# Unnormalised keys in the delta rule: their norm moved into beta and the values

## The chip, the cores and the metric

The kernel runs on one core of a Trainium2 chip. The metric is the device time of one execution in microseconds (us), from several runs of the same program; the time of a kernel is their median. The profile is one further execution, recorded by the hardware profiler. A core has five engines with a queue each: TensorE (PE, with its weight loads shown as PEld), VectorE (DVE), ScalarE (ACT), GpSimd (POOL) and SyncE (SP), which here issues all transfers to the 16 DMA engines.

## The reference

A hybrid decoder layer for 512 tokens of width 2048 in float32: a sliding-window attention branch and a gated delta-rule branch share one wide input projection, are merged by gates, and pass an output projection. The change concerns the delta rule. It has 16 key heads and 32 value heads (two value heads share a key) of width 128. After a causal convolution of four taps and a SiLU, queries and keys are normalised by their Euclidean length and the recurrence is solved in chunks:

```python
def l2_norm(x):
    xf = x.astype(jnp.float32)
    return xf * lax.rsqrt(jnp.sum(xf * xf, axis=-1, keepdims=True) + EPS)
...
    k_beta = k * beta[..., None]
    v_beta = v * beta[..., None]
    L = jnp.where(strict, jnp.einsum('bhncd,bhnsd->bhncs', k_beta, k) * decay, 0.0)
    t_inv = lax.linalg.triangular_solve(eye + L, ...)
    u = t_inv @ v_beta
    w = t_inv @ (k_beta * jnp.exp(g)[..., None])
...
    def step(S, xs):
        u_c, w_c, qk_c, qd_c, kd_c, gl_c = xs
        v_new = u_c - w_c @ S
        o = qd_c @ S + qk_c @ v_new
        S = S * gl_c[..., None, None] + jnp.swapaxes(kd_c, -1, -2) @ v_new
        return S, o
```

The output of each head is normalised by its root mean square, gated, and projected.

## The kernel before

All work hangs on one stream of weight products. A channel tile (`channel_tile`, L290) is 128 output channels by 512 tokens: 16 slices of the inner dimension, three products each (`mm3`, L270), because every float32 operand is split into a high and a low part in a faster 32-bit format. The weights of a tile (1 MB) are loaded by SP into one of two `raw` buffers (L215); ACT rounds a half of it to the high part (L61), DVE subtracts to get the low part (L62), into one of three buffer pairs `whi`/`wlo`. A half serves 24 products. A load or a split is issued when the buffer before it has been used (`half_done`, `weight_tick`).

All other work is written as Python generators that are advanced beside this stream. Every second slice of a channel tile calls `pump` (L91), one step: it counts down each live generator's delay and runs it to its next `yield`, whose value is the number of steps until it goes on. So a step is six weight products, and the order of instructions on each engine follows from these yields, with small rearrangements by the compiler's scheduler. Each engine runs its instructions in its fixed order; a waiting instruction holds up those behind it.

In the key stage (`delta_keys`, L662) 16 channel tiles give the 16 keys; the first four come out of the startup, the next four follow one another, the last eight alternate with tiles of the merge gate. Each key runs through `keys` (L729): convolution and SiLU give y, channels by tokens; y is transposed to tokens by channels (`transpose4`, L317, PSUM tile `ptk`); ACT sums its squares per token (`sumsq`, L774); DVE computes the inverse root by Newton steps (`rsqrt`, L65); ACT writes the normalised keys k with four scaled copies (L745). k is stored for later (L751), transposed back (`ptkT`, L750), copied by ACT to kT (L753), stored (L761) and multiplied with itself on PE (`pkk`, L760). Meanwhile the decay factors E of both value heads are loaded by a broadcast DMA (L783), masked on POOL (L788) and exponentiated on ACT (L794); DVE multiplies them with the product (L763), and six stores (L770, L771) put the result in DRAM. `ptk`, `ptkT` and `pkk` share two buffers in PSUM.

When eight keys are done, `solve` (L796) loads their triangular systems and the rows of beta, scales the systems by beta, and inverts them on DVE in 62 pairs of paced operations. It runs twice.

In the head stage (`delta_heads`, L697) five channel tiles per key head give one query, two values and two output gates. `queries` (L880) loads k and kT, builds the query-key products, and after waiting for both values runs the recurrence (`scan`, L961) over four blocks of 128 tokens. `values` (L869) convolves, transposes into `ptv` and copies with ACT to `vt` (L877), tokens by channels. `neg_beta` (L629) is minus beta, tokens by heads; `queries` uses it at L952. The stores and loads of SP, in its one queue, carry the weights too.

Of the kernel before, what the change touches and what calls it, by code (L numbers as in the profile page):

```python
# [7 lines left out]
F32 = mybir.dt.float32  # L8
F32R = mybir.dt.float32r
I32 = mybir.dt.int32  # L10
AF = mybir.ActivationFunctionType
# [34 lines left out]
class Layer:  # L46
# [615 lines left out]
    def delta_keys(self):  # L662
        tc = self.tc
        dram = self.dram
        self.lt_d = dram.tile([2, 2, 16, 4, HD, HD], F32, name="lt_d")
        self.lab_d = dram.tile([VH, HD, 4, HD], F32, name="lab_d")
        self.ta_d = dram.tile([2, 16, 4, HD, HD], F32, name="ta_d")
        self.ts_d = dram.tile([2, 2, 16, 4, HD, HD], F32, name="ts_d")
        self.kT_d = dram.tile([KH, P, T], F32, name="kT_d")
        self.k_d = dram.tile([KH, P, T], F32, name="k_d")  # L670
        self.o_d = dram.tile([VH, P, T], F32, name="o_d")
        with ExitStack() as sa:
            self.ptp = sa.enter_context(tc.tile_pool(name="ptp", bufs=2, space=PSUM, reuse_waits="tile"))
            self.gwk = sa.enter_context(tc.tile_pool(name="gwk", bufs=1, reuse_waits="tile"))
            wk = sa.enter_context(tc.tile_pool(name="dnA", bufs=2, reuse_waits="tile"))
            gp = sa.enter_context(tc.tile_pool(name="gates", bufs=1, reuse_waits="tile"))
            self.go(self.gates(gp), 1)
            gt = sa.enter_context(tc.tile_pool(name="gatew", bufs=1, reuse_waits="tile"))
            self.beside(self.gate(gt), 0.26, "gate")
            self.keys_done = []  # L680
            for g in range(NST):
                self.go(self.keys(wk, g, self.acc_k[g]), 10 + 8 * g)
            for j in range(NFIRST):
                self.merge_gate("mb", j, self.mb_d)
            self.solved = []
            self.solves = self.paced(self.solve_all(), 0.36)
            for kind, j in self.mixed():
                if kind == "k":
                    self.go(self.keys(wk, j, self.channel_tile(f"k{j}")), 0)
                else:  # L690
                    self.merge_gate("mb", j, self.mb_d)
            for j in range(2):
                self.merge_gate("ma", j, self.ma_d)
            self.drain("gate")
            self.drain_live()
# [33 lines left out]
    def keys(self, wk, g, ps):  # L729

        nc = self.nc
        y = wk.tile([P, T], F32, tag="y", name="y", bufs=3)
        yield from self.conv(wk, ps, 16 + g, y)
        yield 2
        pt = self.ptp.tile([P, T], F32, tag="tp", name="ptk")
        self.transpose4(pt, lambda c: y[:, c * P : (c + 1) * P])
        ss = self.sumsq(wk, pt)
        yield 3
        E = [self.decay_load(wk, 2 * g + e) for e in range(2)]
        nc.vector.tensor_scalar(out=ss, in0=ss, scalar1=EPS, scalar2=None, op0=ALU.add)  # L740
        rk = self.rsqrt(wk, ss, NTB, "rk")
        yield 4
        k = wk.tile([P, NTB, P], F32, tag="k", name="k")
        for c in range(NTB):
            nc.scalar.activation(k[:, c, :], pt[:, c * P : (c + 1) * P], AF.Copy, scale=rk[:, c : c + 1])  # L745
        for e in range(2):
            self.decay_mask(E[e])
        yield 4
        pt = self.ptp.tile([P, T], F32, tag="tp", name="ptkT")
        self.transpose4(pt, lambda c: k[:, c, :])  # L750
        nc.sync.dma_start(out=self.k_d[g], in_=k.rearrange("p c d -> p (c d)"))  # L751
        kT = wk.tile([P, T], F32, tag="kT", name="kT")
        nc.scalar.copy(out=kT, in_=pt)  # L753
        for e in range(2):
            self.decay_exp(E[e], 2 * g + e)
        yield 2
        pk = self.ptp.tile([P, NTB, P], F32, tag="tp", name="pkk")
        for c in range(NTB):
            sl = slice(c * P, (c + 1) * P)
            nc.tensor.matmul(pk[:, c, :], lhsT=kT[:, sl], rhs=kT[:, sl], start=True, stop=True)  # L760
        nc.sync.dma_start(out=self.kT_d[g], in_=kT)  # L761
        for e in range(2):
            nc.vector.tensor_tensor(out=E[e], in0=pk, in1=E[e], op=ALU.mult)  # L763
        yield 2
        for e in range(2):
            h = 2 * g + e
            b, hl = h // 16, h % 16
            for k2 in range(2):
                s = slice(k2 * HD, (k2 + 1) * HD)
                nc.sync.dma_start(out=self.lt_d[b, k2, hl].rearrange("c j i -> j c i"), in_=E[e][s, :, s])  # L770
            nc.sync.dma_start(out=self.lab_d[h], in_=E[e][0:HD, :, HD:P])  # L771
        self.keys_done.append(g)
# [23 lines left out]
    def solve(self, wk, b, eng):  # L796

        nc = self.nc
        while not all(g in self.keys_done for g in range(8 * b, 8 * b + 8)):
            yield 1.0  # L800
        A = wk.tile([P, HD, HD], F32, tag="A", name="A", bufs=1)
        bet = wk.tile([P, HD], F32, tag="bet", name="bet", bufs=1)
        for k2 in range(2):
            s = slice(k2 * HD, (k2 + 1) * HD)
            nc.sync.dma_start(
                out=A[s].rearrange("u j i -> u (j i)"), in_=self.lt_d[b, k2].rearrange("h c j i -> (h c) (j i)")
            )
            nc.sync.dma_start(
                out=bet[s],
                in_=self.b_rows.rearrange("h (c k i) -> k (h c) i", c=4, k=2)[k2, b * HD : (b + 1) * HD, :],  # L810
            )
        yield 8.0
        nb = wk.tile([P, HD], F32, tag="nbet", name="nbet", bufs=1)
        self.behind(eng.tensor_scalar(out=nb, in0=bet, scalar1=-1.0, scalar2=None, op0=ALU.mult))
        self.behind(eng.tensor_tensor(out=A, in0=A, in1=nb.unsqueeze(1).to_broadcast([P, HD, HD]), op=ALU.mult))
        eng.memset(A.rearrange("u j i -> u (j i)")[:, 0 : HD * HD : HD + 1], 1.0)
        for m in range(1, HD - 1):
            n = HD - 1 - m
            yield 0.1 + 0.00115 * m * n
            tmp = wk.tile([P, 1024], F32, tag="atmp", name="atmp", bufs=1)  # L820
            t = tmp[:, : m * n].rearrange("p (j i) -> p j i", j=m)
            self.behind(
                eng.tensor_tensor(  # L823
                    out=t,
                    in0=A[:, m : m + 1, m + 1 :].to_broadcast([P, m, n]),
                    in1=A[:, :m, m : m + 1].to_broadcast([P, m, n]),
                    op=ALU.mult,
                )
            )
            yield 0.1 + 0.00115 * m * n  # L830
            self.behind(eng.tensor_tensor(out=A[:, :m, m + 1 :], in0=A[:, :m, m + 1 :], in1=t, op=ALU.add))  # L831
        tmp = wk.tile([P, 1024], F32, tag="atmp", name="atmp", bufs=1)
        for q in range(8):
            yield 1.1
            half = tmp[:HD, (q % 2) * 512 : (q % 2 + 1) * 512]
            t = half.rearrange("p (i j) -> p i j", j=HD)
            self.behind(nc.scalar.copy(out=t, in_=A[:HD, :, q * 8 : (q + 1) * 8].rearrange("u j i -> u i j")))
            yield 0.2
            nc.sync.dma_start(
                out=self.ta_d[b].rearrange("h c i j -> (h c) (i j)")[:, q * 512 : (q + 1) * 512], in_=half  # L840
            )
        yield 4.5
        self.behind(eng.tensor_tensor(out=A, in0=A, in1=bet.unsqueeze(2).to_broadcast([P, HD, HD]), op=ALU.mult))
        for k2 in range(2):
            s = slice(k2 * HD, (k2 + 1) * HD)
            nc.sync.dma_start(
                out=self.ts_d[b, k2].rearrange("h c j i -> (h c) (j i)"), in_=A[s].rearrange("u j i -> u (j i)")
            )
# [20 lines left out]
    def values(self, wk, g, e, ps, st):  # L869
        nc = self.nc  # L870
        y = wk.tile([P, T], F32, tag="y", name="yv", bufs=3)
        yield from self.conv(wk, ps, 32 + 2 * g + e, y)
        yield 3
        pt = self.ptp.tile([P, T], F32, tag="tp", name="ptv")
        self.transpose4(pt, lambda c: y[:, c * P : (c + 1) * P])
        vt = wk.tile([P, NTB, P], F32, tag="vt", name="vt", bufs=3)
        nc.scalar.copy(out=vt.rearrange("p c d -> p (c d)"), in_=pt)  # L877
        st[f"v{e}"] = vt

    def queries(self, wk, g, ps, st):  # L880
# [926 lines left out]
```

## Time and profile before

| | us |
|---|---|
| median of 3 runs | 2839.93 |
| lowest and highest run | 2839.35, 2842.86 |
| span of the profiled execution (first to last instruction) | 2839.0 |

The profile gives the span of its execution alone; the fastest of the runs is 0.35 us above that span, the median 0.93. The page begins with each engine's busy time, its share of the span and its count of instructions; matmuls overlap, and their ends are modelled. Section 4 of the page is the chain that ended last: from the last instruction back to whatever released it, and so on to the start, as shares of the span. Rows of a timeline give start, duration, engine, line, operation, output<-inputs and count, and in brackets the idle time before with what ended it. A row of a tile gives the durations as minimum/median/maximum in ns, then the first and the last start in us. A row of the waits gives the total in us, the number of times and the longest.

### The profile page before, as it was taken

To read this page: it belongs to the slowest core of one execution; us is meant where nothing else is said; L and a number is where in the kernel's file an instruction comes from. 1 tells how busy PE (TensorE), PEld (TensorE's weight loads), DVE (VectorE), ACT (ScalarE), POOL (GpSimd) and SP (SyncE) were. 2 spreads that over 40 slices of the span, in tenths; PEclk is the share of its full clock that TensorE was granted. 3 is DMA by queue.
4 is the path that set the end of the run, shared out by engine and by line. 5 is a ranking of instruction groups with operands and counts; after the bars stand their busy time and mean duration, and the time that the engine had idled before them with its cause. 6 is when DMAs were issued, how large, how long until landed. Compare 5 with 4: busy or idle time off the path is not lost.

```text
span 2839.0 us, 38354 instructions
## 1 busy us (share of the span) xinstructions
PE 2806.5 (99%) x14152; PEld 2283.3 (80%) x14152; DVE 1944.8 (69%) x3185; ACT 1207.1 (43%) x2476; POOL 146.0 (5%) x124
## 2 busy tenths in 40 slices
PE   8999999999999999999999999999999999999999
PEld 6788888877776788888888888888888888878887
DVE  7866876867758667778766666666656766664676
ACT  5555443244544443333434333333334454432443
POOL 0010000100000010000001000000000000000000
PEclk9999999999999999999999999999999999999999
DMA  9877764322243253356777667677647886885684
GB/s 402 335 246 230 257 218 139 110 91 91 82 135 119 101 168 110 117 201 219 247 255 262 235 224 242 210 239 238 231 167 252 289 314 240 302 273 180 242 318 168
DMA packets 228512, 603.25 MB, mean 212 GB/s; under 512 B 76354, under 2 KB 102594, under 8 KB 188002
## 3 DMA queue, kind: packets, MB, share of 16 engines
q1 hardware_dynamic: 228324, 600.80, 62.1%
q8 instruction: 111, 1.82, 0.3%
q14 instruction: 77, 0.63, 0.1%
HBM read 480.32 MB, written 118.17 MB: 211 GB/s over the span
## 4 chain that ended last, share of the span: by engine, by line
PE 91%; DMA 3%; DVE 3%; ACT 1%; issue 1%; SPq 0%; POOL 0%; DVEq 0%; ACTq 0%; POOLq 0%
PE mm L273 22%; PE mm L275 21%; PE mm L274 21%; PE m L274 5%; PE m L273 5%; PE m L275 5%; PE pod L1000 1%; PE O L1514 1%; PE pv L981 1%; DVE wlo L62 1%; PE pod L999 1%; PE pod L996 1%; PE pp L971 1%; PE S L1451 1%; DMA wa<-in_w_ada_ss 1%
## 5 line engine op out<-in xcount | busy, mean ns | idle before, releaser
L273 PE MATMUL mm<-hh,whi 128*128 128x512 f32 x2784 | 1130.4, 406 | 1.5 <-ACT hh L61 1.5
L275 PE MATMUL mm<-hh,wlo 128*128 128x512 f32 x2784 | 1090.4, 392 | 0.0
L274 PE MATMUL mm<-hl,whi 128*128 128x512 f32 x2784 | 1087.9, 391 | 0.0
L62 DVE TENSOR_TENSOR wlo<-raw,whi 128x1024 fp32r<-128x1024 f32 x516 | 636.9, 1235 | 426.4 <-ACT whi L61 415.4
L61 ACT CAST whi<-raw 128x1024 fp32r<-128x1024 f32 x516 | 541.3, 1050 | 799.9 <-PE mm L274 566.6
L273 PEld LDWEIGHTS mm<-hh,whi 128*128 128x128 f32 x2784 | 524.0, 188 | 117.0 <-issue 14.3
L275 PEld LDWEIGHTS mm<-hh,wlo 128*128 128x128 f32 x2784 | 523.0, 188 | 113.8 <-issue 0.2
L274 PEld LDWEIGHTS mm<-hl,whi 128*128 128x128 f32 x2784 | 524.7, 188 | 100.9 <-issue 1.6
L1246 DVE TENSOR_TENSOR q<-q,q 128x1024 f32<-128x1024 f32 x96 | 124.8, 1300 | 0.0
L794 ACT ACTIVATE E<-E,neg_g 128x128 f32<-128x128 f32 x256 | 81.2, 393 | 92.3 <-POOL E L788 89.6
L831 DVE TENSOR_TENSOR A<-A,atmp 128x62 f32<-128x62 f32 (+30 forms) x124 | 109.5, 883 | 0.6
L823 DVE TENSOR_TENSOR atmp<-A 128x62 f32<-128x62 f32 (+30 forms) x124 | 107.4, 866 | 0.4
L928 POOL TENSOR_TENSOR qe<-qe,yq 128x512 f32<-128x512 f32 x32 | 54.1, 1708 | 923.9 <-DMA qe<-eg_rows 695.9
L1001 ACT COPY osb<-pod 128x256 f32<-128x256 f32 x64 | 23.8, 372 | 152.6 <-PE pod L1000 152.6
L788 POOL TENSOR_SCALAR_AFFINE_SELECT E<-E 128x512 f32<-128x512 f32 x64 | 59.1, 936 | 431.2 <-DMA E<-g_rows 384.5
L983 ACT COPY vn<-pv 128x256 f32<-128x256 f32 x64 | 23.8, 372 | 124.4 <-PE pv L981 124.4
L652 DVE SCALAR_TENSOR_TENSOR yv<-mm,convh,yv 128x511 f32<-128x511 f32 (+2 forms) x96 | 71.2, 742 | 1.1
L988 DVE TENSOR_SCALAR vs<-vn,kd 128x128 f32<-128x128 f32 x96 | 23.1, 283 | 58.3 <-ACT vn L983 58.3
L1482 ACT ACTIVATE sm<-sm,mx,rs 128x128 f32<-128x128 f32 x128 | 61.5, 482 | 3.4 <-DVE mx L1477 2.3
L1011 DVE SCALAR_TENSOR_TENSOR S<-S,egl,pod 128x128 f32<-128x128 f32 x64 | 19.3, 342 | 51.0 <-ACT junk L1004 51.0
L472 DVE SCALAR_TENSOR_TENSOR wa<-wa,silu_cb 128x2048 f32<-128x2048 f32 x22 | 50.1, 2285 | 4.8 <-DMA wa<-in_w_ada_ss 4.8
L657 ACT ACTIVATE th<-yv 128x512 f32<-128x512 f32 x32 | 20.1, 630 | 76.4 <-DVE yv L652 73.7
(444 smaller groups left out, 3678.8 us busy)
## 6 DMA issues: line engine op xcount, KB each, us to landing
raw<-in_w_ch SPq DMA_DIRECT2D x158, 1024.0 KB
wa<-in_w_ada_ss SPq DMA_DIRECT2D x32, 1024.0 KB
q<-in_w_od SPq DMA_DIRECT2D x64, 512.0 KB
g_d<-q SPq DMA_DIRECT2D x64, 512.0 KB
raw<-g_d SPq DMA_DIRECT2D x32, 1024.0 KB
raw<-in_w_od SPq DMA_DIRECT2D x24, 1024.0 KB
gw<-in_w_ada_gate SPq DMA_DIRECT2D x16, 1024.0 KB
E<-g_rows SPq DMA_DIRECT2D x64, 256.0 KB
```

Source lines behind the costliest of these rows:

```text
L61: h = self.nc.scalar.copy(out=hi, in_=src)
L62: l = self.nc.vector.tensor_tensor(out=lo, in0=src, in1=hi.bitcast(F32), op=ALU.subtract)
L273: nc.tensor.matmul(ps, lhsT=wh, rhs=xh, start=first, stop=False)
L274: nc.tensor.matmul(ps, lhsT=wh, rhs=xl, start=False, stop=False)
L275: self.last_mm = nc.tensor.matmul(ps, lhsT=wl, rhs=xh, start=False, stop=last)
L652: nc.vector.scalar_tensor_tensor(out=y[:, s:], in0=ps[:, : T - s], scalar=w[:, j : j + 1], in1=y[:, s:], op0=ALU.mult, op1=ALU.add)
L788: self.last_mask = self.nc.gpsimd.affine_select(out=E, in_=E, pattern=[[0, NTB], [1, P]], compare_op=ALU.is_ge, fill=NEG, base=0, channel_ ...
L794: self.nc.scalar.activation(E[:, c, :], E[:, c, :], AF.Exp, bias=self.neg_g[:, c, h : h + 1])
L823: eng.tensor_tensor(out=t, in0=A[:, m : m + 1, m + 1 :].to_broadcast([P, m, n]), in1=A[:, :m, m : m + 1].to_broadcast([P, m, n]), op=ALU.mult,
L831: self.behind(eng.tensor_tensor(out=A[:, :m, m + 1 :], in0=A[:, :m, m + 1 :], in1=t, op=ALU.add))
L1246: self.behind(nc.vector.tensor_tensor(out=q[f], in0=q[x], in1=q[y], op=ALU.add))
L1482: nc.scalar.activation(t, t, AF.Exp, scale=r[:, h : h + 1], bias=mx[:, h : h + 1], accum_out=den[:, h : h + 1])
```

## The change

Keys are no longer divided by their length. With n the length of a key row (n squared is the sum of squares plus EPS), k = y / n. Beta is divided by n squared, and the values are multiplied by n; the solved quantity then comes out divided by n, and with y in place of k all later products are the same as before. In detail:

- `keys`: the scaled copies, the second transposition and its copy go. ACT copies the transposed y unscaled; y itself takes the place of kT in DRAM and in the self product. y gets four buffers, kT none.
- The length n (`knorm`), as sum times inverse root, stays in SBUF for all keys; the inverse of the sum is multiplied into `neg_beta` and stored for both value heads in `inv_d`, by a transfer that scatters single elements into rows of tokens.
- The yields of `keys` after the sum of squares: 3, 2, 2, 2, 2 instead of 3, 4, 4, 2, 2.
- `solve` loads the rows of `inv_d` beside those of beta and multiplies them.
- `values`: four scaled copies instead of one copy.

```diff
+        self.inv_d = dram.tile([VH, T], F32, name="inv_d")
+        self.knorm = self.dnc.tile([P, NTB, KH], F32, name="knorm")
...
     def keys(self, wk, g, ps):
 
         nc = self.nc
-        y = wk.tile([P, T], F32, tag="y", name="y", bufs=3)
+        y = wk.tile([P, T], F32, tag="y", name="y", bufs=4)
         yield from self.conv(wk, ps, 16 + g, y)
         yield 2
         pt = self.ptp.tile([P, T], F32, tag="tp", name="ptk")
         self.transpose4(pt, lambda c: y[:, c * P : (c + 1) * P])
+        nc.sync.dma_start(out=self.kT_d[g], in_=y)
         ss = self.sumsq(wk, pt)
+        k = wk.tile([P, NTB, P], F32, tag="k", name="k")
+        nc.scalar.copy(out=k.rearrange("p c d -> p (c d)"), in_=pt)
         yield 3
         E = [self.decay_load(wk, 2 * g + e) for e in range(2)]
         nc.vector.tensor_scalar(out=ss, in0=ss, scalar1=EPS, scalar2=None, op0=ALU.add)
         rk = self.rsqrt(wk, ss, NTB, "rk")
-        yield 4
-        k = wk.tile([P, NTB, P], F32, tag="k", name="k")
-        for c in range(NTB):
-            nc.scalar.activation(k[:, c, :], pt[:, c * P : (c + 1) * P], AF.Copy, scale=rk[:, c : c + 1])
+        nc.vector.tensor_tensor(out=self.knorm[:, :, g], in0=ss, in1=rk, op=ALU.mult)
+        inv = wk.tile([P, NTB], F32, tag="inv", name="inv")
+        nc.vector.reciprocal(out=inv, in_=ss)
+        both = inv.unsqueeze(2).to_broadcast([P, NTB, 2])
+        nb = self.neg_beta[:, :, 2 * g : 2 * g + 2]
+        nc.vector.tensor_tensor(out=nb, in0=nb, in1=both, op=ALU.mult)
+        nc.sync.dma_start(out=self.k_d[g], in_=k.rearrange("p c d -> p (c d)"))
+        for e in range(2):
+            nc.sync.dma_start(out=self.inv_d[2 * g + e].rearrange("(c p) -> p c", p=P), in_=inv)
+        yield 2
         for e in range(2):
             self.decay_mask(E[e])
-        yield 4
-        pt = self.ptp.tile([P, T], F32, tag="tp", name="ptkT")
-        self.transpose4(pt, lambda c: k[:, c, :])
-        nc.sync.dma_start(out=self.k_d[g], in_=k.rearrange("p c d -> p (c d)"))
-        kT = wk.tile([P, T], F32, tag="kT", name="kT")
-        nc.scalar.copy(out=kT, in_=pt)
+        yield 2
         for e in range(2):
             self.decay_exp(E[e], 2 * g + e)
         yield 2
         pk = self.ptp.tile([P, NTB, P], F32, tag="tp", name="pkk")
         for c in range(NTB):
             sl = slice(c * P, (c + 1) * P)
-            nc.tensor.matmul(pk[:, c, :], lhsT=kT[:, sl], rhs=kT[:, sl], start=True, stop=True)
-        nc.sync.dma_start(out=self.kT_d[g], in_=kT)
+            nc.tensor.matmul(pk[:, c, :], lhsT=y[:, sl], rhs=y[:, sl], start=True, stop=True)
...
         bet = wk.tile([P, HD], F32, tag="bet", name="bet", bufs=1)
+        nb = wk.tile([P, HD], F32, tag="nbet", name="nbet", bufs=1)
...
-            nc.sync.dma_start(
-                out=bet[s],
-                in_=self.b_rows.rearrange("h (c k i) -> k (h c) i", c=4, k=2)[k2, b * HD : (b + 1) * HD, :],
-            )
+            for dst, rows in ((bet, self.b_rows), (nb, self.inv_d)):
+                nc.sync.dma_start(
+                    out=dst[s], in_=rows.rearrange("h (c k i) -> k (h c) i", c=4, k=2)[k2, b * HD : (b + 1) * HD, :]
+                )
         yield 8.0
-        nb = wk.tile([P, HD], F32, tag="nbet", name="nbet", bufs=1)
+        self.behind(eng.tensor_tensor(out=bet, in0=bet, in1=nb, op=ALU.mult))
...
         vt = wk.tile([P, NTB, P], F32, tag="vt", name="vt", bufs=3)
-        nc.scalar.copy(out=vt.rearrange("p c d -> p (c d)"), in_=pt)
+        for c in range(NTB):
+            nc.scalar.activation(vt[:, c, :], pt[:, c * P : (c + 1) * P], AF.Copy, scale=self.knorm[:, c, g : g + 1])
```

## The prediction

> **What bounds the kernel now.** I read the page first, then the windows of the key stage, then PE's timeline in it.
>
> ```profile
> span 2839.0 us, 38354 instructions
> ...
> PE 2806.5 (99%) x14152; PEld 2283.3 (80%) x14152; DVE 1944.8 (69%) x3185; ACT 1207.1 (43%) x2476; POOL 146.0 (5%) x124
> ...
> PE 91%; DMA 3%; DVE 3%; ACT 1%; issue 1%; SPq 0%; POOL 0%; DVEq 0%; ACTq 0%; POOLq 0%
> ```
>
> PE is busy for 2806.5 of 2839.0 us, and the chain that ended last lies on PE for 91%. The change works in the key stage (about 140 to 445 us) and where values leave PSUM in the head stage. In the windows the columns are the length, the busy time (and count) of PE, PEld, DVE, ACT and POOL, PE's clock, the DMA share and GB/s:
>
> ```profile
> 140.00:200.00 60.00, 60.00 (x300) 49.78 (x300) 41.31 (x79) 33.03 (x99) 6.78 (x8) 1.00 0.72 237
> 200.00:260.00 60.00, 58.99 (x296) 48.84 (x295) 39.94 (x92) 39.96 (x120) 6.63 (x9) 1.00 0.72 224
> 260.00:320.00 60.00, 60.00 (x287) 49.95 (x287) 40.45 (x70) 28.38 (x69) 4.26 (x6) 1.00 0.84 266
> 320.00:380.00 60.00, 60.00 (x283) 49.91 (x282) 51.91 (x82) 29.99 (x79) 6.63 (x6) 1.00 0.77 257
> 380.00:445.00 65.00, 65.00 (x301) 52.73 (x301) 44.13 (x67) 25.65 (x60) 4.15 (x6) 1.00 0.52 174
> ```
>
> PE misses only 1.0 us of these 305, at a granted clock of 1.00. So an instruction taken off PE here shortens the run as long as nothing else comes late, and work added to ACT, DVE, SP or the DMA queues costs nothing until PE waits for it.
>
> **What leaves PE.** Each of the 16 keys loses its second transposition, four matmuls of 128x128, 64 in all. The tile's row gives min/median/max in ns; the timeline shows one such group between weight products; the last two rows are the ends of a run without any insertion:
>
> ```profile
> L320 PE MATMUL ptkT<-ident,k x64: 270/273/330, 165.0 to 435.7; 128*128 128x128 f32 x64
> ...
> 290.10 0.39 PE L274 MATMUL mm<-hl,whi 128*128 128x512 f32 x1
> 290.32 0.40 PE L275 MATMUL mm<-hh,wlo 128*128 128x512 f32 x1
> 290.56 0.60 PE L320 MATMUL ptkT<-ident,k 128*128 128x128 f32 x4
> 290.91 0.48 PE L273 MATMUL mm<-hh,whi 128*128 128x512 f32 x1
> 291.23 0.40 PE L274 MATMUL mm<-hl,whi 128*128 128x512 f32 x1
> 291.46 0.39 PE L275 MATMUL mm<-hh,wlo 128*128 128x512 f32 x1
> ...
> 302.42 0.39 PE L275 MATMUL mm<-hh,wlo 128*128 128x512 f32 x1
> ...
> 312.62 0.39 PE L275 MATMUL mm<-hh,wlo 128*128 128x512 f32 x1
> ```
>
> From 302.42 to 312.62 there are 45 products: 10.20 / 45 = 0.227 us from start to start, though each row lasts 0.39 (they overlap). From the L275 at 290.32 to the next at 291.46 are 1.14 us, where three products alone take 0.68. The group therefore costs PE 1.14 - 0.68 = 0.46 us. 16 x 0.46 = **7.4 us** leave PE. I price by the displacement and not by the 273 ns, since neighbours overlap.
>
> The Trainium skill ("TensorE: Matmul & The Clock Gate", Part 4) gives about 275 ns for one PE transposition inside a kernel. The trace agrees on the duration (273); by the page the sum would be 64 x 0.275 = 17.6 us. That is the third rival below.
>
> A second gain is a wait. In this stage PE waits on ACT once:
>
> ```profile
> PE ptk L320 <- ACT k L745: 0.9, 1, 0.9
> ```
>
> The two transposition buffers in PSUM are shared by three tiles per key, and one is held until ACT has scaled it by the root, which DVE must compute first. After the change the copy needs no root and there are two tiles per key: this wait should go, **0.9 us**. What is late next is taken up below.
>
> The products of the keys with themselves (L760) stay, eight entries per key, reading y instead of kT; same shape and count, no cost.
>
> **What is added and moved.** DVE gets three small operations per key (norm, reciprocal, new beta) and one multiplication per solve.
>
> ```profile
> L73 DVE TENSOR_TENSOR rkt<-rkt,ss x48: 149/161/585, 155.6 to 422.7; 128x4 f32<-128x4 f32 x48
> ...
> L1487 DVE RECIPROCAL den<-den x16: 202/203/204, 581.5 to 1002.8; 128x8 f32<-128x8 f32 x16
> ```
>
> 2 x 0.16 + 0.20 = 0.52 us per key, 8.4 us in all, spread over a stage where DVE is at most 51.91 of 60 us busy: hidden. Uncovered it would be those 8.4 us.
>
> ACT loses the copy of the transposed keys and three of the four scaled copies in the key stage, and gets three more per value tile in the head stage:
>
> ```profile
> L753 ACT COPY kT<-ptkT x16: 567/587/606, 166.3 to 436.0; 128x512 f32<-128x512 f32 x16
> ...
> 210.05 1.14 ACT L745 ACTIVATE k<-ptk,rky 128x128 f32<-128x128 f32 x4 [0.98 <-DVE rky L74]
> ...
> 1077.48 0.58 ACT L877 COPY vt<-ptv 128x512 f32<-128x512 f32 x1
> ...
> L981 PEld LDWEIGHTS pv<-vt,tt x40: 187/189/193, 1080.9 to 1693.5; 128*128 128x128 f32 x40
> ```
>
> Four scaled pieces take 1.14 us where one copy takes 0.58, so 32 value tiles cost ACT 32 x 0.56 = 18 us more. The first product that needs a value tile starts at 1080.9, 2.8 us after that copy ended at 1078.06; 0.56 more fits. Hidden; a tile that didn't fit would cost at most 0.56, 18 us at the very worst.
>
> The new order in a key: between the first transposition and the self product lie 9 steps of the generator instead of 13 (3+2+2+2 for 3+4+4+2). The decay factors E keep the time of their load, but mask, exponential and product come 2, 4 and 4 steps sooner.
>
> ```profile
> 298.75 0.60 PE L320 MATMUL ptk<-ident,y 128*128 128x128 f32 x4
> ...
> 305.68 0.91 SPq L783 DMA_DIRECT2D E<-g_rows  x2
> ...
> 312.15 1.30 POOL L788 TENSOR_SCALAR_AFFINE_SELECT E<-E 128x512 f32<-128x512 f32 x2 [19.13 <-DMA E<-g_rows]
> ...
> 315.93 2.46 ACT L794 ACTIVATE E<-E,neg_g 128x128 f32<-128x128 f32 x8
> ...
> 317.63 0.89 PE pkk L760 x8
> ```
>
> 13 steps took 317.63 - 298.75 = 18.9 us, 1.45 each. With 9 the self product stands at 298.75 + 13.1 = 311.8. But the mask waits for the load until 312.15 and ends at 313.45, and eight exponentials take 2.46: E is whole at about 315.9. So DVE would stand at its product for 2 to 4 us, and ACT at its exponential, issued at step 7 (308.9), for some 4 us. Behind them queue the split of the weights (L61 on ACT, L62 on DVE), the next convolution and the solver; PE waits for the split. Its cover:
>
> ```profile
> 306.01 1.05 ACT L61 CAST whi<-raw 128x1024 fp32r<-128x1024 f32 x1 [3.44 <-PE mm L274]
> ...
> 307.10 1.23 DVE L62 TENSOR_TENSOR wlo<-raw,whi 128x1024 fp32r<-128x1024 f32 x1
> ```
>
> The cast waits for PE to free the buffer it just finished, so with three buffers two halves are ready: 2 x 24 x 0.227 = 10.9 us of PE work, and the split is done at 308.33, 2.3 us after the start. A cover of 8.6 us against a delay of 2 to 4. It is thinner where DVE is at 51.91 of 60. I bound PE's new waits by 0 and by 5 us (four keys in 320 to 400 at a good microsecond each) and take **+1.0**, near the only such row there is (0.9).
>
> SP and the queues. The stores of keys move forward; that of the transposed form (L761) now waits for nothing new. Two stores per key are new, 512 runs of 4 bytes each. They are issued right behind DVE's chain, so SP stands there until DVE has run it, with weight loads behind; a load has the same cover.
>
> ```profile
> L751 SPq DMA_DIRECT2D k_d<-k x16: 319/383/601, 164.3 to 425.1; - x16
> ...
> L770 SPq DMA_DIRECT2D lt_d<-E x64: 574/611/1827, 172.7 to 444.1; - x64
> ```
>
> A store of 128 runs is issued in 383 ns, one of 256 runs in 611; carried on, 512 take about 1.1 us (estimate), 2.2 per key. No row shows a 4-byte run written to DRAM. Nearest below is a window with only short reads, nearest above one with 256-byte stores:
>
> ```profile
> DMA packets 307, 0.01 MB, mean 10 GB/s; under 512 B 307, under 2 KB 307, under 8 KB 307
> ...
> q1 hardware_dynamic: 307, 0.01, 14.5%
> ```
>
> ```profile
> DMA packets 933, 0.33 MB, mean 304 GB/s; under 512 B 880, under 2 KB 880, under 8 KB 932
> ...
> q1 hardware_dynamic: 932, 0.32, 115.4%
> ```
>
> The first (461.0 to 462.2) gives 0.145 x 16 x 1.2 us / 307 = 9 ns a run, the second (279.5 to 280.6) 1.154 x 16 x 1.1 / 932 = 22 ns. 1024 runs per key on 16 engines are 0.6 to 1.4 us per key. From 200 to 260 the share is 0.72, so 28% of the time is free; a key comes there with each channel tile at most, 48 x 0.227 = 10.9 us, so 3.1 us are free per key. So it is hidden; I take 9 to 22 ns, because the rows for the shorter and the longer run bracket the size, and keep the other price as the second rival. Two more loads per half in the solver are of 64 rows and lie beside the load of A.
>
> **The sum**, on the execution's span: 2839.0 - 7.4 - 0.9 + 1.0 = 2831.7. The median of the runs, 2839.93, lies 0.9 above the span: **2832.6 us**.
>
> **Rivals.**
> First, the wait moves instead of going: E comes too late for the shorter order, DVE and ACT stall at every key, and where DVE is fullest the split of the weights is late. For it: mask at 312.15 against a product at 311.8. Against it: 8.6 us of cover. At the upper bound, +5: 2836.6.
>
> Second, slower: the 4-byte stores fill the queues, and weights and E come late. It decides from the point where 1024 runs eat the free 3.1 us of a key: 3.1 x 16 / 1024 = 48 ns a run in the dense stretch, and from 80 ns for the whole stage (free by the five windows' shares: 0.28 x 120 + 0.16 x 60 + 0.23 x 60 + 0.48 x 65 = 88 us less the last keys' share, some 82; 16384 runs on 16 engines). At 100 ns the runs take 102 us, 20 over: 2839.9 - 8.3 + 20 = 2852. Against it stand the 9 and 22 ns. The Trainium skill ("DMA: Bandwidth & Descriptors", Specifications) says that transfers under 512 bytes are done by reading, modifying and writing back. It gives no price for it; the trace's 256-byte stores show none at 22 ns, and no row here shows one at 4 bytes.
>
> Third, PE gets back the transpositions' whole duration: 64 x 0.273 = 17.5 us, 2839.9 - 17.5 - 0.9 + 1.0 = 2822.5. The displacement of 0.46 per group speaks against it.
>
> **How the numbers follow.** The forecast (2830 to 2834) has 0.66, the first rival 0.17, the slow one 0.11, the third 0.06. The measurement can tell about 0.2% from no change, 5.7 us: faster is below 2834.3, slower above 2845.6. Faster: 0.66 + 0.06 = 0.72; same 0.17; slower 0.11. The range starts at the forecast without the new wait (2831.6) less 2.6 us, a quarter of the way to the third rival, since single groups may be displaced differently, and ends 2 us above the first rival: 2829 to 2838.5.
>
> **What would show it.** Right: 64 fewer matmuls on PE; busy time of PE lower by about 7; the stage from the first key to the last product of the stage shorter by 7 to 8; no PE wait on ACT at ptk; the value copies at 1.14 us with PE's product still behind them by over 2 us. The first rival: PE waits on wlo or whi between 200 and 440, DVE idle before L763's product. The second: DMA share near 1 there, casts waiting for raw. The prediction is wrong if the stage's PE time falls by 7 and the end doesn't follow, which would mean that something behind this stage sets the end.

## The result and the profile after

The changed kernel takes 2886.2 us (median of 4 runs, 2884.57 to 2891.89) against 2840.21 us (4 runs, 2839.35 to 2842.86) for the kernel before in the same comparison. The ratio is 1.0164, with a 95% interval of 1.0149 to 1.0178: slower by 46 us. I had forecast 2832.6 and given the case that came true, the second rival, a chance of 0.11.

The head of the page of the changed kernel: span, busy time of the engines, PE's clock and the DMA share in 40 slices of 72 us, and the chain that ended last.

```profile
span 2884.0 us, 38324 instructions
...
PE 2809.8 (97%) x14088; PEld 2285.4 (79%) x14088; DVE 1947.6 (68%) x3235; ACT 1209.9 (42%) x2508; POOL 140.0 (5%) x124
...
PEclk9999899999999999999999999999999999999999
DMA  9889998332235243346777767667646887885684
...
PE 84%; DMA 9%; DVE 3%; issue 2%; ACT 1%; SPq 1%; POOL 0%; DVEq 0%; POOLq 0%; ACTq 0%
```

PE has its 64 matmuls fewer (14152 to 14088), yet its busy time is 3.3 us longer, and the chain, which lay on PE for 91%, has 9% on DMA where it had 3%. Both point to one stage. The windows of the key stage after the change (length, then busy time and count of PE, PEld, DVE, ACT, POOL, then PE's clock, DMA share, GB/s):

```profile
140.00:200.00 60.00, 57.52 (x271) 46.79 (x269) 32.15 (x72) 25.54 (x76) 4.95 (x6) 0.97 0.75 170
200.00:260.00 60.00, 41.92 (x181) 34.28 (x180) 31.27 (x84) 23.92 (x65) 3.82 (x6) 0.85 0.89 179
260.00:320.00 60.00, 53.94 (x246) 44.79 (x246) 30.69 (x70) 24.21 (x66) 4.94 (x6) 0.93 0.96 166
320.00:380.00 60.00, 52.78 (x223) 42.86 (x224) 45.78 (x77) 21.48 (x49) 3.17 (x4) 0.88 1.00 239
380.00:445.00 65.00, 55.42 (x249) 45.25 (x247) 44.95 (x72) 25.18 (x59) 4.72 (x6) 0.95 0.99 209
445.00:500.00 55.00, 52.79 (x231) 42.55 (x232) 40.67 (x66) 19.84 (x48) 4.06 (x6) 0.97 0.87 219
```

PE is full at clock 1.00 in the same windows before. Now it misses up to 18 us of 60, and its clock falls to 0.85. The DMA share rises to as much as 1.00, while in the first four windows the bytes per second fall (from 380 us on, the late work is still being loaded). Over the whole stretch from 140 to 500 us no engine but the queues works longer. That stretch as one window, first before, then after:

```profile
140.00:500.00 360.00, 358.99 (x1706) 296.74 (x1706) 253.55 (x429) 176.63 (x448) 28.45 (x34) 1.00 0.66 217
```

```profile
140.00:500.00 360.00, 314.36 (x1398) 256.52 (x1397) 225.51 (x436) 140.17 (x362) 25.67 (x34) 0.92 0.91 197
```

By the durations of their packets the queues are busy for 0.25 x 360 = 90 us longer, and they move a tenth less. PE stands for 45.6 us instead of 1.0, and the trace's clock records give 54.6 us at half clock, where before had none. Matched product by product, the weight products run 54 us later than before's at 490 us, 47 later at 885, and 45 later at the end: the whole loss is made in the key stage, and some 9 us come back afterwards.

PE's waits after the change, from 140 to 500 us (what waited, for what; us in total, times, longest):

```profile
PE ptk L320 <- DVE y L659: 25.6, 6, 8.3
PE ptk L320 <- DVE rky L74: 9.1, 1, 9.1
PE mm L273 <- ACT whi L61: 5.2, 2, 3.2
PE mm L275 <- DVE wlo L62: 3.6, 4, 1.1
```

The list names DVE, yet DVE has less to do than before. The timeline shows who is really late (start, duration, engine, line, operation; in brackets the idle time ahead and what ended it):

```profile
190.81 1.06 SPq L755 DMA_DIRECT2D inv_d<-inv  x2
...
195.06 0.43 SPq L788 DMA_DIRECT2D E<-g_rows  x1
...
206.70 0.64 POOL L793 TENSOR_SCALAR_AFFINE_SELECT E<-E 128x512 f32<-128x512 f32 x1 [10.43 <-DMA lab_d<-E]
...
207.37 0.40 ACT L799 ACTIVATE E<-E,neg_g 128x128 f32<-128x128 f32 x1 [7.43 <-DMA lab_d<-E]
207.67 0.61 ACT L657 ACTIVATE th<-y 128x512 f32<-128x512 f32 x1
208.32 0.69 DVE L659 SCALAR_TENSOR_TENSOR y<-th,y 128x512 f32<-128x512 f32 x1 [6.36 <-ACT th L657]
209.16 1.09 PE L320 MATMUL ptk<-ident,y 128*128 128x128 f32 x4 [9.12 <-DVE rky L74]
...
210.90 0.63 PE L275 MATMUL mm<-hh,wlo 128*128 128x512 f32 x1
```

Read upwards from PE: it stands 9.12 us for y; DVE stands 6.36 for the convolution's tanh; that tanh is queued on ACT behind the exponential of E, which stands 7.43; the exponential needs POOL's mask, which stands 10.43 for E's load. The brackets of the mask and the exponential name the store of `lab_d`, but the semaphore of that load of E, for which the mask also waits, is complete only at 206.40, 0.3 us before the mask. The load was issued at 195.06, and the mask begins 11.6 us later; in the case of before quoted in the prediction it was 6.5 (305.68 to 312.15). The load left SP behind the two stores of 190.81. Nothing on this path computes longer: each engine works in order, so one late load stops all of them.

A second loss follows the stall: the last row lasts 0.63 us where such products lasted 0.39. PE works at half clock after it.

### The profile page after: what moved, and what is told of

Same layout as the page of the kernel before. It is cut to its first block, busy times and chain, and to the rows that moved or that the text cites. A ratio compares the mean times of both kernels' runs of the same rounds, so it can differ in the third digit from the quotient of the medians.

```text
span 2884.0 us, 38324 instructions
## 1 busy us (share of the span) xinstructions
PE 2809.8 (97%) x14088; PEld 2285.4 (79%) x14088; DVE 1947.6 (68%) x3235; ACT 1209.9 (42%) x2508; POOL 140.0 (5%) x124
## 4 chain that ended last, share of the span: by engine, by line
PE 84%; DMA 9%; DVE 3%; issue 2%; ACT 1%; SPq 1%; POOL 0%; DVEq 0%; POOLq 0%; ACTq 0%
PE mm L273 20%; PE mm L275 19%; PE mm L274 19%; PE m L274 5%; PE m L273 5%; PE m L275 5%; DMA gw<-in_w_ada_gate 3%; DMA E<-g_rows 2%; DMA raw<-in_w_ch 2%; PE pv L988 1%; PE pod L1007 1%; PE O L1521 1%; DMA mb_d<-mth 1%; PE pod L1006 1%; PE pod L1003 1%
## 5 line engine op out<-in xcount | busy, mean ns | idle before, releaser
L1717 DVE SCALAR_TENSOR_TENSOR gate_bc<-gw,silu_c,gate_bc 128x2048 f32<-128x2048 f32 x15 | 35.6, 2375 | 26.6 <-DMA gw<-in_w_ada_gate 26.6
```

## The experiments

| run | us, median | before, same chip | ratio (95%) | DMA share 140 to 500 |
|---|---|---|---|---|
| e1_no_scatter | 2824.28 | 2842.02 | 0.9939 (0.9921 to 0.9956) | 0.65 |
| e2_before_scatter | 2891.60 | 2842.02 | 1.0160 (1.0128 to 1.0191) | 0.91 |
| e3_rows_by_pe | 2831.44 | 2842.02 | 0.9964 (0.9952 to 0.9976) | 0.65 |
| e4_old_yields | 2900.15 | 2842.02 | 1.0205 (1.0186 to 1.0225) | 0.90 |
| e5_one_store | 2900.61 | 2840.53 | 1.0209 (1.0193 to 1.0226) | 0.89 |
| e6_runs_16 | 2843.80 | 2840.53 | 1.0009 (1.0000 to 1.0019) | 0.69 |
| e7_runs_apart | 2845.14 | 2840.53 | 1.0016 (1.0006 to 1.0025) | 0.70 |
| e8_rows_old_yields | 2847.99 | 2840.53 | 1.0026 (1.0016 to 1.0037) | 0.65 |
| e9_rows_paused | 2845.75 | 2838.45 | 1.0023 (1.0012 to 1.0034) | 0.66 |
| e10_runs_16_bytes_apart | 2848.16 | 2838.45 | 1.0032 (1.0020 to 1.0044) | 0.78 |
| e11_change_runs_apart | 2831.33 | 2840.07 | 0.9971 (0.9960 to 0.9982) | 0.75 |

**Is it the stores, and are they enough?** Two kernels from both ends: the changed kernel without its stores, and the kernel before with nothing but them.

e1_no_scatter, against the changed kernel:

```diff
-        for e in range(2):
-            nc.sync.dma_start(out=self.inv_d[2 * g + e].rearrange("(c p) -> p c", p=P), in_=inv)
...
-            for dst, rows in ((bet, self.b_rows), (nb, self.inv_d)):
+            for dst, rows in ((bet, self.b_rows),):
...
-        self.behind(eng.tensor_tensor(out=bet, in0=bet, in1=nb, op=ALU.mult))
+        self.behind(eng.tensor_scalar(out=bet, in0=bet, scalar1=0.001, scalar2=None, op0=ALU.mult))
```

> The changed kernel without the 32 scattering stores of 4-byte runs; the solver multiplies beta by 0.001 in place of the loaded inverse, so its result is another. Everything else of the change stays: the shorter order, the unscaled copy, the scaled values. Theory S (the scattering stores hold the DMA queues, and weights and E come late): about 2832 us, PE idle under 3 us between 140 and 500 us, DMA share near 0.66 there. Theory O (the shorter order and the moved stores stall ACT, DVE and SP whatever the stores cost): about 2880 us, PE idle still some 45 us.

e2_before_scatter, against the kernel before, behind the root of a key (nothing reads what it stores):

```diff
+        self.inv_d = dram.tile([VH, T], F32, name="inv_d")
...
         rk = self.rsqrt(wk, ss, NTB, "rk")
+        inv = wk.tile([P, NTB], F32, tag="inv", name="inv")
+        nc.vector.reciprocal(out=inv, in_=ss)
+        for e in range(2):
+            nc.sync.dma_start(out=self.inv_d[2 * g + e].rearrange("(c p) -> p c", p=P), in_=inv)
```

> The kernel before, with one reciprocal per key and the 32 scattering stores added after the inverse root; nothing reads them. Theory S: slower than before by 40 to 55 us, the cost of the stores without the gain of the dropped transposition, so 2880 to 2895. Theory O: within 3 us of before, about 2841, because the old order is kept.

Without stores the change gains 17.7 us (0.9939); the stores alone cost the kernel before 49.6 us (1.0160; its four runs spread from 2878.85 to 2898.89, and the interval allows 36 to 54 us). The key stage in one window, and PE's only wait in it, for the changed kernel without stores:

```profile
140.00:500.00 360.00, 359.62 (x1680) 297.53 (x1679) 266.82 (x488) 162.15 (x386) 33.88 (x34) 1.00 0.65 216
```

```profile
PE ptk L320 <- DVE y L659: 0.4, 1, 0.4
```

And for the kernel before with stores the window and the longest of PE's waits:

```profile
140.00:500.00 360.00, 319.57 (x1473) 261.12 (x1472) 218.84 (x402) 158.03 (x429) 23.86 (x34) 0.95 0.91 197
```

```profile
PE pkk L765 <- ACT kT L758: 29.6, 4, 11.8
```

In the changed order without stores PE waits 0.4 us; in the old order with stores it waits again, at another place, and the share is the 0.91 of the changed kernel. The loss goes with the stores and not with the order. At 490 us the first stands 9.9 us ahead of the kernel before, the second 52.1 behind.

**Is it the order after all?** The first rival said that the decay factors come too late for the shorter pauses. e4_old_yields gives the changed kernel the old pauses and keeps the stores.

```diff
-        yield 2
+        yield 4
         for e in range(2):
             self.decay_mask(E[e])
-        yield 2
+        yield 4
```

> The changed kernel with the two old pauses of 4 steps in place of 2 before the mask and before the exponential, so that E has its old distance from its load; the scattering stores stay. Theory S: 2880 to 2890 us, no more than 6 us from the changed kernel. Theory O: most of the loss gone, 2835 to 2850.

It came out at 2900.15 (1.0205), not better than the changed kernel's 1.0164. That refutes the order as the cause of the loss, but it is also above the 2880 to 2890 expected: the old pauses make this kernel slower still. e8_rows_old_yields makes the same edit on e3_rows_by_pe (below), where no short stores disturb it:

> The lengths brought into rows by PE, no scattering stores, with the two old pauses of 4 steps. If the shorter order by itself costs PE waits of some microseconds (the first rival of the prediction), this is faster than the form with short pauses (2831.4): 2825 to 2830. If the order is free, the same within 3 us.

It is 2847.99 (1.0026) where the short pauses have 0.9964: the old pauses are some 17 us worse in this kernel. Neither expectation held, and it is the opposite of the first rival. PE's waits in its key stage:

```profile
PE ptk L320 <- DVE y L659: 3.1, 1, 3.1
PE pkk L764 <- DVE E L766: 2.8, 1, 2.8
PE mm L275 <- DVE wlo L62: 1.8, 1, 1.8
PE mm L273 <- ACT whi L61: 0.8, 1, 0.8
```

8.6 us of idle time, with 6.8 us at half clock. Why the longer order makes them wasn't isolated.

**What makes the stores dear?** Three things were possible: that SP stands behind DVE's chain when it issues them, with loads behind it; that so many runs cost their time; or that the runs lie close together. All four kernels below are e2 with one edit, so SP issues at the same place behind the same chain. One store per key instead of two:

```diff
-        for e in range(2):
-            nc.sync.dma_start(out=self.inv_d[2 * g + e].rearrange("(c p) -> p c", p=P), in_=inv)
+        nc.sync.dma_start(out=self.inv_d[2 * g].rearrange("(c p) -> p c", p=P), in_=inv)
```

> The kernel before with one reciprocal and one scattering store per key instead of two: 16 stores, 8192 runs of 4 bytes, read by nothing. If the stores' runs are the price, between a quarter and two thirds of the loss of the two-store form (49.6 us by the medians): 2855 to 2875 us. If the loss came from SP standing at a store until DVE has run its chain, the single store stands there as long, and the loss stays near 50 us: about 2890.

The same 2 KB, but a partition's four values side by side (128 runs of 16 bytes in place of 512 of 4):

```diff
-self.inv_d[2 * g + e].rearrange("(c p) -> p c", p=P)
+self.inv_d[2 * g + e].rearrange("(p c) -> p c", p=P)
```

> The kernel before with the reciprocal and two stores per key of the same bytes, but laid out so that each partition writes one run of 16 bytes: 128 runs per store, 4096 in all, in an order nothing reads. If the price is per run, a quarter of the runs: 2842 to 2856 us. If it is per byte or per store, about 2890.

The same 512 runs of 4 bytes, 64 bytes apart:

```diff
-        self.inv_d = dram.tile([VH, T], F32, name="inv_d")
+        self.inv_d = dram.tile([VH, T, 16], F32, name="inv_d")
...
-self.inv_d[2 * g + e].rearrange("(c p) -> p c", p=P)
+self.inv_d[2 * g + e, :, 0].rearrange("(c p) -> p c", p=P)
```

> The kernel before with the reciprocal and two stores per key of 512 runs of 4 bytes, as in the changed kernel, but each run 64 bytes from the next in DRAM, so that no two neighbours share a 64-byte line; read by nothing. If neighbouring runs in one line hold each other up, most of the loss goes: 2842 to 2860. If every short write has the price by itself: 2880 to 2900.

And 16 bytes apart (`[VH, T, 4]` in the same edit):

> The kernel before with the reciprocal and two stores per key of 512 runs of 4 bytes, each run 16 bytes from the next, so that four share 64 bytes; read by nothing. Runs 64 bytes apart gave 2845.1, runs side by side 2891.6. If any sharing of a line is the price, a large part of the loss comes back: 2855 to 2890. If only close neighbours hold each other up, about 2845.

The pair e2 and e7 decides it: same count of runs, same bytes, same issuing place, 32 stores each; 49.6 us lost when the runs lie side by side, 4.6 when they are 64 bytes apart. Sixteen bytes apart lose 9.7, one 16-byte run per partition 3.3. This excludes SP's standing (at the same place in all of them) and the count of runs as the cause of the loss. Sixteen bytes apart came out between its two expectations. e8 above and e9 below show that a small change of order moves this kernel by 14 to 17 us, so the few microseconds of e6, e7 and e10 say less than their shares (0.69, 0.70, 0.78). One store per key lost 60.1 us, no less than two. By its expectation that would speak for SP's standing, but e6 and e7 exclude that; it shows that the price isn't a fixed one of each run (90 us of queue time for e2's 16384 runs are 88 ns a run, 83 us for e5's 8192 are 162). The two stores of a key do run side by side: in e2 they are issued 0.47 us apart and complete 0.29 us apart (medians). Why half of the runs hold up the queues about as long as all of them stays open.

The jam itself can be seen in the queues. First the 8 us after the first stores of e2 (153.5 to 161.5 us; busy share in tenths and GB/s in 40 slices of 0.2 us, each packet counted whole in the slice in which it starts; then packets, MB and share):

```profile
DMA  9936996799999978878699998990000000990743
GB/s 389 267 92 215 174 102 61 133 246 307 297 197 188 229 206 166 106 85 196 215 277 256 92 92 92 72 10 0 0 0 0 0 0 0 51 61 10 123 82 31
...
q1 hardware_dynamic: 1611, 1.02, 105.9%
```

Then the same 8 us of e7:

```profile
DMA  9454462689999899976986394219296184777789
GB/s 389 164 205 143 113 102 102 236 328 278 259 228 248 167 218 147 156 206 266 297 236 154 123 379 174 102 61 123 92 266 92 41 307 174 266 328 328 328 369 451
...
q1 hardware_dynamic: 1756, 1.73, 83.0%
```

In e2 the rate falls to 92, to 10 and then to 0 for seven slices. The busy share stays at 8 to 9 down to the slice with 10 GB/s; then no packet starts for 1.4 us. Sixteen packets of 2 KB that start between 157.60 and 158.76, right behind most of the short ones, last 1.8 to 6.3 us each, where the median of their size is 84 ns. Even a load of E that was issued at 153.18, ahead of the stores, is caught: POOL's second mask, which waits for it, begins 10.9 us after its issue, while with e7's layout the masks of both loads of that pair are done by 158.74:

```profile
164.10 0.64 POOL L793 TENSOR_SCALAR_AFFINE_SELECT E<-E 128x512 f32<-128x512 f32 x1 [6.35 <-DMA E<-g_rows]
```

Over the 8 us the packets that start in e2 hold 1.02 MB, those in e7 1.73. The short packets' own records don't show the price. In the changed kernel's trace, over the key stage, a 4-byte packet lasts 11.6 ns on average, and a 256-byte one 18.0 (17.7 before). But the 2 KB packets last 175.7 ns instead of 93.0, their 99th percentile is 2700 instead of 272, and the 8 KB packets last 518 instead of 376. Whoever prices such a store by its packets' own time reads 12 ns; the bill is on the packets beside and behind it. The longest packet that starts within 8 us of a store's issue has a median of 6.4 us in the changed kernel, 5.9 in e2, 2.0 in e10, 1.3 in e6 and 1.1 in e7. The semaphores tell it of the stores themselves: from issue to completion they take 12.7 us in the changed kernel, 13.7 in e2, 11.9 in e5, 8.4 in e10, 6.7 in e6 and 6.2 in e7 (medians).

**Can the change be had without the jam?** e3_rows_by_pe drops the short stores and turns the lengths of eight keys into rows on PE, once per solve:

```diff
+        pr = self.ptp.tile([P, T], F32, tag="tp", name="pinv")
+        for x in range(NTB):
+            nc.tensor.transpose(pr[0:8, x * P : (x + 1) * P], self.knorm[:, x, 8 * b : 8 * b + 8], self.ident)
+        rows = wk.tile([P, 1024], F32, tag="atmp", name="nrows", bufs=1)[0:8, 0:T]
+        nc.vector.tensor_copy(out=rows, in_=pr[0:8])
+        for e in range(2):
+            nc.sync.dma_start(out=self.inv_d.rearrange("(g e) t -> e g t", e=2)[e, 8 * b : 8 * b + 8], in_=rows)
...
+        self.behind(eng.reciprocal(out=nb, in_=nb))
+        self.behind(eng.tensor_tensor(out=bet, in0=bet, in1=nb, op=ALU.mult))
         self.behind(eng.tensor_tensor(out=bet, in0=bet, in1=nb, op=ALU.mult))
```

> The change with the lengths brought into rows by PE: when eight keys are done, four transpositions of 128x8, one copy on DVE and two stores of 8 rows of 2 KB replace the 32 scattering stores; the solver loads those rows and takes the reciprocal, squared, there. Theory S: 2832 to 2835 us, faster than before by 5 to 8, for PE pays about 2 x 0.4 us for the transpositions. Theory O: about 2880.

2831.44 us, 0.9964: faster than before by 10.6 us, a little more than expected. e9_rows_paused adds a `yield 1.5` between the row stores and the loads that read them, since SP stood between the two:

> The form with rows by PE (2831.4 us), with a pause of 1.5 units of the solver's budget (some four steps, about 6 us) between the store of the rows and the loads that read it. In the form without it SP stood from 258.1 to 260.5 us until the rows had landed, with the next weights behind it, and PE waited on whi and wlo at 282 to 285. If that is what it lost against the form without any rows (2824.3), this one comes to 2824 to 2829 us. If not, 2830 to 2834.

It missed: 2845.75 (1.0023), slower than without the pause. The pause cut SP's standing before the loads from 2.4 us to 0.9, yet PE still waits for the split weights at 286 to 288 us. SP's standing there wasn't what made those waits; what did is open. Last, e11_change_runs_apart is the changed kernel with e7's layout: `[VH, T, 16]`, stored to and read from `[..., 0]`, and nothing else.

```diff
-        self.inv_d = dram.tile([VH, T], F32, name="inv_d")
+        self.inv_d = dram.tile([VH, T, 16], F32, name="inv_d")
...
-            nc.sync.dma_start(out=self.inv_d[2 * g + e].rearrange("(c p) -> p c", p=P), in_=inv)
+            nc.sync.dma_start(out=self.inv_d[2 * g + e, :, 0].rearrange("(c p) -> p c", p=P), in_=inv)
...
-            for dst, rows in ((bet, self.b_rows), (nb, self.inv_d)):
+            for dst, rows in ((bet, self.b_rows), (nb, self.inv_d[:, :, 0])):
```

> The changed kernel as it is, but the runs of its 32 scattering stores lie 64 bytes apart in DRAM; the solver reads them there, 64 runs of 4 bytes per partition in place of one of 256 bytes. If sharing of lines is what made the change slow: the gain of the form without stores (-17.7 us) less what the stores apart cost on the kernel before (4.6) and less the longer loads of the solver, 2828 to 2842 us. If the changed kernel is slow for another reason too: above 2860.

Its page has a span of 2829.7 us; its key stage in one window, and PE's waits there:

```profile
140.00:500.00 360.00, 352.41 (x1637) 291.24 (x1635) 262.86 (x478) 159.06 (x381) 32.94 (x34) 0.99 0.75 215
```

```profile
PE ptk L320 <- DVE y L659: 3.7, 1, 3.7
PE pkk L766 <- ACT k L742: 2.1, 1, 2.1
PE mm L275 <- DVE wlo L62: 1.6, 1, 1.6
```

2831.33 us, 0.9971 (0.9960 to 0.9982): inside the expected range. With sixteen times the room in DRAM for one small array, the slow change becomes a kernel that beats the one before by 0.3%. The waits of 45.6 us are down to 7.4 in all.

## Why the prediction was wrong

**The step that failed** is the price of a 4-byte run: "I take 9 to 22 ns, because the rows for the shorter and the longer run bracket the size". The stage's share gave 90 us for 16384 runs on 16 engines, 88 ns each, above both of the thresholds that the prediction had worked out for its second rival (48 ns in the dense stretch, 80 for the stage). Two things were wrong with the bracket. A row of short reads and a row of 256-byte stores say nothing of short writes that lie side by side; spacing, which neither row varied, is what decided. And I read the packets' own durations, which stay near 10 ns even when the store holds up everything behind it. With the runs 64 bytes apart the bracket does hold by the share: e7's share is 0.70, so 0.04 x 360 x 16 / 16384 = 14 ns a run.

The Trainium skill ("DMA: Bandwidth & Descriptors", Specifications) says that transfers under 512 bytes are done by reading, modifying and writing back. Neighbours that hold one another up would fit that; but e7's runs are as far under 512 bytes as e2's and cost a sixth by the share, so that rule alone doesn't give the price, and no run here shows the mechanism behind it.

**The second rival** had the direction right, and both of its signs are there: a share of up to 1.00, and casts that wait for `raw` (ACT, 7 times, 32.5 us from 140 to 500 us; none before). But its chance (0.11) and its price (2852) were too low, and the price alone wasn't its fault: at the measured 88 ns its own rule gives 90 - 82 = 8 us of overflow and 2839.9 - 8.3 + 8 = 2840, where the run took 2886. That is a second step that failed: the free share of the queues was taken as cover that a store may use up. Behind a store of e2 single packets stood for up to 6.3 us, so a load came late however much of the stage was free, and the engines, which work in order, passed the delay on. PE's half clock comes on top. What turns 90 us of queue time into 54 of PE's is that chain.

**Point by point.**
- The transpositions leave PE: right, and so is their size. Matched product by product, fifteen of the sixteen groups in the trace of before set the weight products back by the same 0.46 us as the one quoted; the sixteenth is split in two. Without stores (e1) the end of the key stage comes 9.9 us sooner: 1.0 of that is there at 160 us, ahead of the first group, 0.6 is idle time (1.0 to 0.4), 7.4 are the groups, and 0.9 wasn't located. The third rival would have needed 1.09 per group.
- PE's wait for ACT's scaled copy goes: right in e1, whose list has one wait of 0.4 us, on another engine. In e11 a wait on ACT's copy is back, at the self product (2.1 us).
- New waits of +1.0: right for the bare order (0.4 us in e1), too small with any stores and loads. e11 has 7.6 us of idle time in the stage and 6.8 at half clock, and stands at 490 us only 0.1 us ahead of the kernel before, where e1 stands 9.9 ahead.
- The first rival: refuted by e1 (same order, 0.4 us of waits), and by e4 and e8 (longer pauses, slower). The waits on whi and wlo that I had named as its sign are in the changed kernel, but as a result of the stores: a sign that both rivals share tells nothing.
- DVE's additions and the value copies are hidden: right. DVE's busy time rose by 2.8 us. A value tile's four scaled copies take the 1.14 us that the key's did, and PE's product still starts over 2 us after them:

```profile
1123.80 1.14 ACT L884 ACTIVATE vt<-ptv,knorm 128x128 f32<-128x128 f32 x4
...
L988 PEld LDWEIGHTS pv<-vt,tt x64: 187/190/192, 1127.2 to 2142.4; 128*128 128x128 f32 x64
```

- Issue of the stores: estimated 2.2 us for the two of a key, measured about half of that (min/median/max in ns):

```profile
L755 SPq DMA_DIRECT2D inv_d<-inv x32: 371/509/1327, 153.2 to 475.4; - x32
```

**What wasn't in the sum.** The forecast (2832.6) and e11 (2831.33) agree in part by chance. e11's gain in the key stage is nearly used up by its waits; 7.6 us come between 490 and 885 us, of which the prediction had nothing. There the kernel before has an idle PE and a half clock that the changed one lacks. The window from 800 to 900 us before, and with e11's layout:

```profile
800.00:900.00 100.00, 97.64 (x516) 71.21 (x515) 63.09 (x139) 41.59 (x96) 5.31 (x4) 0.98 0.40 111
```

```profile
800.00:900.00 100.00, 98.85 (x555) 75.25 (x554) 72.03 (x160) 43.30 (x100) 5.19 (x4) 1.00 0.44 121
```

1.2 us less idle time and 3.4 us less at half clock (1.7 us lost) are about 3 of these 7.6. All of the 7.6 arises between 840 and 890 us, where the attention's products lie among the weight products in another order; the rest wasn't explained.

## What to carry to other kernels

Price a scattering store by how close its runs lie in DRAM and by what stands behind it in the queues, never by its packets' own durations: 4-byte writes side by side cost this kernel 50 us, the same writes 64 bytes apart 5. When a page shows DMA share up and GB/s down in one stage, look for new small writes there before looking at the engines that the waits name. And where a kernel is full on PE, count beside a wait of a few microseconds the slow clock that can follow it: here 45.6 us of waits cost 16.5 us more.

## What the runs showed of the hardware

**Spacing of short writes.** 512 runs of 4 bytes 4, 16 and 64 bytes apart raised the stage's share by 0.25, 0.12 and 0.04. Only these three spacings ran, so where the effect ends between 16 and 64 bytes, or beyond, isn't known.

**PE's clock can fall after short waits.** In the kernel before, PE stands for under 2 us between 863 and 865 us, and its clock is halved for one step of 3.4 us soon after:

```profile
863.00:865.00 2.00, 0.34 (x6) 0.00 (x0) 0.70 (x4) 2.00 (x8) 0.00 (x0) 1.00 0.01 4
865.00:866.30 1.30, 1.28 (x8) 0.77 (x9) 1.30 (x8) 0.26 (x1) 0.00 (x0) 1.00 0.00 0
866.30:869.70 3.40, 3.40 (x15) 1.14 (x14) 2.43 (x5) 2.17 (x5) 0.00 (x0) 0.52 0.02 5
```

In the clock records of these traces every half-clock stretch but the last of a trace is a whole number of steps of 3.413 us. In all of them, from 140 us on, no wait of under 1.5 us that stands alone (no other within 12 us) is followed by such a step, and every one of over 3 us is. Between the two the length doesn't decide: 1.60 us at 870 us of e10 brought a step, 2.75 us at 302 us of e9 and 2.99 us at 476 us of e2 brought none. What decides there isn't shown. The changed kernel's 45.6 us of idle time brought 54.6 us at half clock. Of these, 21.5 us lie in the waits themselves; the other 33.1 us cost half of it, 16.5 us of work. Idle time of 44.6 us more than before and these 16.5, less the 7.4 of the transpositions, are 53.7 us, near the 54 by which the products are late at 490 us. The Trainium skill ("TensorE: Matmul & The Clock Gate", HAM oscillation — how this bites in real kernels) gives the rule that PE should have no gaps over about 3.4 us; the length of the step agrees, but here gaps of half that were sometimes enough.
